# Two weight sums of a fast matrix product move from VectorE into accumulating transfers

## The chip, the cores and the metric

The kernel runs on one core of one Trainium2 chip. A core has TensorE (PE, matrix products into PSUM), VectorE (DVE), ScalarE (ACT), GpSimd (POOL) and SyncE (SP); SP issues most transfers, POOL the accumulating ones, and 16 DMA engines carry them all. The metric is the device time of one execution in microseconds. Before the change the median of three runs is 2101.67 us (2101.33 to 2106.94).

## The reference

One encoder layer on 512 tokens of width 2048, all in float32:

```
xn   = rms_norm(x)
proj = xn @ w_in                               # 2048 x 5120: conv value, gate, q, k, v
y_c  = silu(layer_norm(dwconv31(val * sigmoid(gate))))
y_n  = neighbourhood attention(q, k, v)        # 8 x 64 grid, window 8 x 16, 16 heads
x    = x + concat(rms_norm(y_c), rms_norm(y_n)) @ w_out
xn   = rms_norm(x)
up   = dwconv3(xn @ w_up)                      # 2048 x 11264
gate, val = split(up)
x    = x + (silu(gate) * val) @ w_down         # 5632 x 2048
out  = rms_norm(x)
```

The change touches only how `xn @ w_up` gets its weights.

## The kernel before, in words

**Layout.** Activations stand transposed: 16 tiles of 128 channels by 512 tokens. Every weight comes in units of 128 partitions x 1024 columns (512 KB), which are eight 128x128 blocks. For float32 accuracy, `parts` (L106) cuts each raw unit in two: ACT rounds it into `whi` (L109), VectorE forms the remainder `wlo` (L110). `mm3` (L117) then does three matmuls per block: high by high (L120), high by low (L121), low by high (L122). A unit is thus 24 matmuls.

**Stages.** The input projection (tiles `pj`) runs with convolution and attention beside it, then the output projection (`po`), then the gated MLP, then the last down products with the final norm. In the MLP the up projection is `up(f)` (L581), for 44 columns f in 11 chunks of four. For each f it forms 128 gate channels and 128 value channels for all 512 tokens at once. This is a 2x2 block product by seven multiplications instead of eight (Strassen-Winograd): the inner dimension is cut in halves, the 512 tokens in halves of 256, and the weights of f in four quarters, A11, A21, A22, A12, each one unit of 512 KB in HBM. The activation's combinations (`comb`, L485 to L516) are made once. The weights' combinations are made for each f by `factors` (L528): product 0 uses A22, product 1 uses A21 + A22, product 2 uses A21 + A11, product 3 uses A11, product 4 uses s = A21 + A22 + A11, product 5 uses A12, and product 6 uses s + A12 (signs are in the activations and in the negated value path `fwn`). So there are four additions of quarters per f, all on VectorE: L539, L541, L546, L550, each over 128x1024 numbers. `up` adds the seven products (PSUM tiles `pu`) with ACT (L602, L606) and VectorE (L605 to L611); `hidden` multiplies by the norm's factor (L627, L628), does the width-3 convolution `conv3` (L619 to L621), silu (L630) and the gate product (L631).

**Down products.** While chunk c runs up, the down projection of chunk c-1 runs between its products: `down` (L640) takes a unit of `w_down` for two output tiles; ACT copies each PSUM tile `pd` to `pdc` (L649), and POOL adds it to the residual in HBM by an accumulating transfer (`x2d`, L650). `down_units` (L559) says after which product: in the chunks 1 to 9 one unit after product 3 and one after product 6, so that a column is nine units; in chunk 0 there are none, and in the last chunk none in its first column.

**Order and buffers.** `plan` is the list of all weight units in the order of use, each a function that makes its parts; `weights()` (L141) hands out the next one and makes units three ahead (`AHEAD`). Raw units and sums share one pool of seven tiles (tag `raw`, `NR`), the parts have four tiles each (`NW`). Products 0 to 5 share three PSUM tiles (`psm`), product 6 has one of its own. The instructions of each engine are put in order by a planner from the program's order and estimated durations; on the chip each engine runs its own list in order and waits on semaphores, and a transfer's issue stands in its queue's order (SP's or POOL's) until its buffer is free.

Of the kernel before, what the change touches and what calls it, by code (L numbers as in the profile page):

```python
# [13 lines left out]
ALU = mybir.AluOpType  # L14
AX = mybir.AxisListType

P = 128
# [17 lines left out]
U = 8  # L35
# [8 lines left out]
NT = 79  # L44
NR = 7
AHEAD = 3
NW = 4
NEG = -1.0e30

# [15 lines left out]
def layer(ctx: ExitStack, tc: tile.TileContext, xT, w_in, w_out, w_up, w_down, par, tab, out):  # L65
    nc = tc.nc
# [19 lines left out]
    def t4(shape, name):  # L86

        return wpool.tile(shape, F32, tag="raw", name=name, bufs=NR)
# [13 lines left out]
    def raw_unit(src, n):  # L102
        raw = t4([P, U * P], "raw")
        return raw, nc.sync.dma_start(raw[:, :n], src)

    def parts(raw, n):  # L106
        hi = wpool.tile([P, U * P], F32R, tag="whi", name="whi", bufs=NW)
        lo = wpool.tile([P, U * P], F32R, tag="wlo", name="wlo", bufs=NW)
        i = nc.scalar.activation(hi[:, :n], raw[:, :n], AF.Copy)  # L109
        j = nc.vector.tensor_sub(lo[:, :n], raw[:, :n], hi[:, :n].bitcast(F32))  # L110
        return hi, lo, i, j
# [27 lines left out]
    plan, made = [], []  # L139

    def weights():  # L141
        at = weights.at
        weights.at += 1
        while len(made) < min(at + 1 + AHEAD, len(plan)):
            made.append(plan[len(made)]())
        return made[at]

    weights.at = 0

# [56 lines left out]
    for k in range(KD):  # L206
# [6 lines left out]
        if k in (0, 2, 6, 15):  # L213
            raw, i = raw_unit(first[len(early)], U * P)
# [8 lines left out]
    for step in ORDER:  # L223
        i = next(a_ if step == "a" else q_)
# [18 lines left out]
    def project(n):  # L243
        ps = psm.tile([P, S], F32, tag="mm", name="pj")
        for u in range(KD // U):
            w = weights()
            for k in range(U):
                kk = u * U + k
                m = mm3(ps, w, k, xs[kk][0], xs[kk][1], kk == 0, kk == KD - 1)
            tick(m)  # L250
            while late:
                late.pop()()
        return ps
# [200 lines left out]
    def out_half(m, read):  # L454
        for d in range(KD):
            w = weights()
            ps = psm.tile([P, S], F32, tag="mm", name="po2")
            for k in range(U):
                i = mm3(ps, w, k, m[k][0], m[k][1], k == 0, k == U - 1)
            tick(i)  # L460
            read(d, ps)
# [66 lines left out]
    def factors(f):  # L528

        def load(q):  # L530
            a[q] = raw_unit(w_up[f, q], U * P)[0]
            return a[q]

        def make(c):
            if c == 0:
                return load(A22)
            if c == 1:
                a["s"] = t4([P, U * P], "ws")
                add(a["s"], load(A21), a[A22])  # L539
            elif c == 2:  # L540
                add(a[A21], a[A21], load(A11))  # L541
                return a[A21]
            elif c == 3:
                return a[A11]
            elif c == 4:
                add(a["s"], a["s"], a[A11])  # L546
            elif c == 5:
                return load(A12)
            else:
                add(a["s"], a["s"], a[A12])  # L550
            return a["s"]

        a = {}
        return [lambda c=c: parts(make(c), U * P)[:2] for c in range(7)]

    A11, A21, A22, A12 = range(4)
    add = nc.vector.tensor_add
# [13 lines left out]
    for c in range(NCH):  # L571
        for i in range(CH):
            for at, make in enumerate(factors(c * CH + i)):
                plan.append(make)
                for d0 in down_units(c, i, at):
                    plan.append(lambda c=c, d0=d0: unit(down_weights((c - 1) * CH, d0), U * P))
# [4 lines left out]
    def up(f, between):  # L581

        def product(c):
            w = weights()
            ps = (psa.tile([P, S], F32, tag="po", name="pu") if c == 6 else
                  psm.tile([P, S], F32, tag="mm", name="pu"))[:, :H]
            for k in range(U):
                m = comb[c][k]
                i = mm3(ps, w, k, m[:, :H], m[:, H:], k == 0, k == U - 1)
            tick(i)  # L590
            between(c)
            return ps
# [78 lines left out]
    ws = []  # L671
# [89 lines left out]
```

## Time and profile before

| | |
|---|---|
| runs | 2101.67 us median (2101.33 to 2106.94) |
| profiled execution | span 2106.4 us |
| TensorE | 2067.0 us busy, 98% |
| VectorE | 1575.8 us busy, 75% |
| ScalarE | 988.8 us busy, 47% |
| GpSimd | 140.1 us busy, 7% |
| chain of waits | TensorE 96%, VectorE 2%, DMA 1%, ScalarE 1% |
| transfers | 270.89 MB, mean 129 GB/s |

The profile is one execution. "Busy" of TensorE counts pipelined matmuls whose ends are modelled. A row of instruction groups gives line, engine, operation, output and inputs with their sizes, the count, the busy time, the mean ns of one, and the idle time of the engine just before, with what ended it. In the timeline, `[3.05 <-DMA raw<-in_w_up]` says that the engine stood 3.05 us before this instruction and that the named thing let it go. PEclk is the granted TensorE clock, 1.00 at full speed.

### The profile page before, as it was taken

The numbers are of one execution on the slowest core, as the hardware profiler recorded it, in microseconds if no ns is written. First come the engines' busy times: TensorE is split into PE (matmuls) and PEld (weight loads), VectorE is DVE, ScalarE is ACT, GpSimd is POOL, SyncE is SP. The second block draws the span as 40 slices with busy tenths as digits, with TensorE's granted clock in tenths as the row PEclk, the third lists the DMA queues.
The fourth block names the chain that finished last, engine by engine and source line by source line (L and its number), as shares of the span: only waits on it lengthen the run. The fifth ranks groups of instructions, "written<-read, shape, count | busy, mean of one in ns | idle before, by whom it ended". The sixth has DMA issues, their size and how long they took to land.

```text
span 2106.4 us, 32366 instructions
## 1 busy us (share of the span) xinstructions
PE 2067.0 (98%) x13024; PEld 1853.7 (88%) x13024; DVE 1575.8 (75%) x2137; ACT 988.8 (47%) x1472; POOL 140.1 (7%) x166
## 2 busy tenths in 40 slices
PE   8999999999999999999999999999999999999997
PEld 6888888877878899999999999999999999998986
DVE  7986796686568897777777777777776777768666
ACT  6144424456436554454544544454454445444442
POOL 0000000000000001110111101101001011010110
PEclk9999999999999999999999999999999999999998
DMA  6233223236224235565565555556656556553672
GB/s 226 90 121 100 92 89 105 99 108 213 97 96 135 80 121 135 127 138 141 122 142 138 135 136 141 130 131 145 138 127 141 141 131 131 140 135 99 145 203 81
DMA packets 95910, 270.89 MB, mean 129 GB/s; under 512 B 10640, under 2 KB 14736, under 8 KB 95760
## 3 DMA queue, kind: packets, MB, share of 16 engines
q1 hardware_dynamic: 72720, 226.88, 34.4%
q0 software_dynamic: 23040, 41.95, 14.4%
q8 instruction: 102, 1.67, 0.3%
q14 instruction: 48, 0.39, 0.1%
HBM read 218.46 MB, written 50.33 MB: 128 GB/s over the span
## 4 chain that ended last, share of the span: by engine, by line
PE 96%; DVE 2%; DMA 1%; ACT 1%; issue 0%; SPq 0%; DVEq 0%; ACTq 0%
PE pu L120 14%; PE pu L122 14%; PE pu L121 14%; PE pd L122 8%; PE pd L120 8%; PE pd L121 8%; PE pj L120 7%; PE pj L122 7%; PE pj L121 7%; PE po L120 3%; PE po L121 3%; PE po L122 3%; PE sc L366 1%; PE po L409 1%; PE trp L396 1%; DMA raw<-in_w_up 1%
## 5 line engine op out<-in xcount | busy, mean ns | idle before, releaser
L110 DVE TENSOR_TENSOR wlo<-raw,whi 128x1024 fp32r<-128x1024 f32 x368 | 449.3, 1222 | 361.8 <-ACT whi L109 336.6
L120 PE MATMUL pu<-xc,whi 128*128 128x256 f32 x2464 | 699.8, 284 | 8.2 <-ACT vv L602 4.7
L122 PE MATMUL pu<-xc,wlo 128*128 128x256 f32 x2464 | 699.5, 284 | 0.0
L121 PE MATMUL pu<-xc,whi 128*128 128x256 f32 x2464 | 699.5, 284 | 0.0
L109 ACT ACTIVATE whi<-raw 128x1024 fp32r<-128x1024 f32 x368 | 389.2, 1059 | 627.7 <-PE pj L121 217.1
L120 PEld LDWEIGHTS pu<-xc,whi 128*128 128x128 f32 x2464 | 474.5, 193 | 12.8 <-ACT vv L602 4.9
L121 PEld LDWEIGHTS pu<-xc,whi 128*128 128x128 f32 x2464 | 474.6, 193 | 3.5 <-issue 0.4
L122 PEld LDWEIGHTS pu<-xc,wlo 128*128 128x128 f32 x2464 | 474.5, 193 | 0.0
L650 POOL DMA_DIRECT2D x2d<-pdc x160 | 139.4, 873 | 1902.0 <-ACT pdc L649 1794.1
L120 PE MATMUL pj<-xh,whi 128*128 128x512 f32 x640 | 254.0, 398 | 7.7 <-ACT whi L109 7.7
L120 PE MATMUL pd<-hh,whi 128*128 128x512 f32 x640 | 250.3, 391 | 1.9 <-ACT pdc L649 1.9
L122 PE MATMUL pj<-xh,wlo 128*128 128x512 f32 x640 | 250.6, 392 | 0.7 <-DVE wlo L110 0.6
L121 PE MATMUL pj<-xl,whi 128*128 128x512 f32 x640 | 251.2, 393 | 0.0
L121 PE MATMUL pd<-hl,whi 128*128 128x512 f32 x640 | 250.3, 391 | 0.0
L122 PE MATMUL pd<-hh,wlo 128*128 128x512 f32 x640 | 248.9, 391 | 0.0
L109 ACT ACTIVATE whi<-ws 128x1024 fp32r<-128x1024 f32 x132 | 139.9, 1060 | 192.9 <-PE pu L121 135.1
L280 DVE SCALAR_TENSOR_TENSOR y<-ch,prm,y 128x507 f32<-128x507 f32 (+14 forms) x240 | 170.1, 741 | 3.1
L110 DVE TENSOR_TENSOR wlo<-ws,whi 128x1024 fp32r<-128x1024 f32 x132 | 161.3, 1222 | 12.4 <-ACT whi L109 11.8
L649 ACT ACTIVATE pdc<-pd 128x512 f32<-128x512 f32 x160 | 94.0, 588 | 133.4 <-PE pd L122 133.3
L120 PEld LDWEIGHTS pj<-xh,whi 128*128 128x128 f32 x640 | 120.8, 189 | 36.1 <-ACT whi L109 9.0
L122 PEld LDWEIGHTS pj<-xh,wlo 128*128 128x128 f32 x640 | 120.7, 189 | 27.7 <-DVE wlo L110 2.1
L122 PEld LDWEIGHTS pd<-hh,wlo 128*128 128x128 f32 x640 | 120.3, 188 | 28.1 <-DVE wlo L110 3.4
(141 smaller groups left out, 2452.7 us busy)
## 6 DMA issues: line engine op xcount, KB each, us to landing
raw<-in_w_up SPq DMA_DIRECT2D x176, 512.0 KB, 3.5
raw<-in_w_down SPq DMA_DIRECT2D x88, 512.0 KB, 4.0
raw<-in_w_in SPq DMA_DIRECT2D x80, 512.0 KB, 3.7
x2d<-pdc POOLq DMA_DIRECT2D x160, 256.0 KB, 4.7
raw<-in_w_out SPq DMA_DIRECT2D x32, 512.0 KB, 3.4
x<-in_xT SPq DMA_DIRECT2D x32, 256.0 KB, 6.0
tab<-in_tab SPq DMA_DIRECT2D x32, 256.0 KB, 4.0
x2d<-x SPq DMA_DIRECT2D x16, 256.0 KB, 2.0
```

The lines of the kernel that those rows point to most:

```text
L109: i = nc.scalar.activation(hi[:, :n], raw[:, :n], AF.Copy)
L110: j = nc.vector.tensor_sub(lo[:, :n], raw[:, :n], hi[:, :n].bitcast(F32))
L120: nc.tensor.matmul(ps, hi[:, a], mh, start=start, stop=False)
L121: nc.tensor.matmul(ps, hi[:, a], ml, start=False, stop=False)
L122: return nc.tensor.matmul(ps, lo[:, a], mh, start=False, stop=stop)
L280: nc.vector.scalar_tensor_tensor(y[:, a:b], h[:, a + j - PAD:b + j - PAD], prm[:, o + j:o + j + 1], y[:, a:b], op0=ALU.mult, op1=ALU.add)
L366: m = nc.tensor.matmul(both[:, j, i, :], q[hp, b * P:(b + 1) * P], grid(k, KC0[b], KW)[hp], start=True, stop=True)
L396: m = nc.tensor.transpose(ps[:, 2 * i + ch, :], s[:, i, ch * P:(ch + 1) * P], ident)
L409: m = nc.tensor.matmul(grid(po, b * BLK, BLK)[hp], vt[b // 2][:, 2 * (b % 2) + ch, hp], pts[j][:, 2 * i + ch, :], start=(ch == 0), stop=(c ...
L649: nc.scalar.activation(t, ps, AF.Copy)
L650: nc.gpsimd.dma_start(xd[d], t, accum_op=ALU.add)
```

## The change

Two of the four additions are no longer done on VectorE: A21 + A22 (L539, for product 1) and A21 + A11 (L541, for product 2). In their place one quarter is loaded into a raw tile by SP, and POOL issues a second transfer from HBM that adds the other quarter to the tile in SBUF. Both are begun eight units ahead of the product that uses them (`FAR`), by a table `sums` that `weights()` looks up. Product 1 splits the summed tile directly, and the additions for product 4 (L546, now L556) and product 6 (L550, now L560) go on in the same tile on VectorE. Since the tiles of A22 and A11 are no longer shared with the additions, A22 and A11 are loaded a second time as plain operands. So a column loads five quarters plainly, where it loaded four, and adds two by accumulating transfers. Seven raw tiles are allocated per column with down units, as before (there, one of them for `ws`).

```
+FAR = 8
     def weights():
         at = weights.at
         weights.at += 1
+        for i in range(at, min(at + 1 + FAR, len(plan))):
+            sum_ = sums.pop(i, None)
+            if sum_ is not None:
+                sum_()
         while len(made) < min(at + 1 + AHEAD, len(plan)):
             made.append(plan[len(made)]())
         return made[at]
+
+    sums = {}
...
+        def summed(q1, q2):
+            t = load(q1)
+            nc.gpsimd.dma_start(t, w_up[f, q2], accum_op=ALU.add)
+            return t
+
         def make(c):
             if c == 0:
                 return load(A22)
             if c == 1:
-                a["s"] = t4([P, U * P], "ws")
-                add(a["s"], load(A21), a[A22])
+                return a["s"]
             elif c == 2:
-                add(a[A21], a[A21], load(A11))
                 return a[A21]
             elif c == 3:
-                return a[A11]
+                return load(A11)
             elif c == 4:
                 add(a["s"], a["s"], a[A11])
             elif c == 5:
...
         a = {}
+
+        def ahead(c):
+            a["s" if c == 1 else A21] = summed(*((A22, A21) if c == 1 else (A21, A11)))
+
+        for c in (1, 2):
+            sums[len(plan) + c] = lambda c=c: ahead(c)
         return [lambda c=c: parts(make(c), U * P)[:2] for c in range(7)]
```

## The prediction

> **What bounds the kernel now.** I read the page first, then stretches of the span, then the few places where TensorE stood. The page gives the engine times, the DMA queues and the issues:
>
> ```profile
> span 2106.4 us, 32366 instructions
> PE 2067.0 (98%) x13024; PEld 1853.7 (88%) x13024; DVE 1575.8 (75%) x2137; ACT 988.8 (47%) x1472; POOL 140.1 (7%) x166
> q1 hardware_dynamic: 72720, 226.88, 34.4%
> q0 software_dynamic: 23040, 41.95, 14.4%
> x2d<-pdc POOLq DMA_DIRECT2D x160, 256.0 KB, 4.7
> raw<-in_w_up SPq DMA_DIRECT2D x176, 512.0 KB, 3.5
> ```
>
> TensorE is busy 98% of the span and VectorE 75%. The stretches tell more (columns: us; busy time of PE, PEld, DVE, ACT, POOL; granted TensorE clock; DMA share; GB/s):
>
> ```profile
> 708.00:712.00 4.00, 0.54 (x4) 0.23 (x2) 3.90 (x13) 1.41 (x3) 0.00 (x0) 1.00 0.09 14
> 712.83:716.24 3.41, 3.41 (x16) 3.15 (x15) 0.79 (x2) 0.60 (x1) 0.00 (x0) 0.50 0.60 210
> 1916.00:1921.00 5.00, 0.40 (x4) 0.19 (x2) 5.00 (x8) 3.36 (x7) 0.00 (x0) 1.00 0.37 105
> 1921.15:1924.56 3.41, 3.41 (x16) 3.41 (x17) 3.41 (x5) 0.16 (x1) 0.00 (x0) 0.50 0.00 0
> 2021.00:2025.00 4.00, 2.09 (x10) 1.40 (x9) 3.68 (x7) 3.27 (x6) 0.57 (x1) 1.00 0.99 354
> 1200.00:1400.00 200.00, 200.00 (x1387) 187.21 (x1387) 145.48 (x171) 94.86 (x125) 22.63 (x26) 1.00 0.59 136
> ```
>
> ```profile
> 700.00:2000.00 1300.00, 1291.76 (x9076) 1214.77 (x9075) 979.40 (x1167) 628.16 (x839) 132.37 (x152) 1.00 0.56 132
> ```
>
> In the steady part (1200 to 1400) TensorE is busy all 200 us at the full clock. VectorE does 145 us of work beside it, so nothing that VectorE is spared there can come off the time. In all of 700 to 2000, the up projection's stage, TensorE is idle for 1300 - 1291.76 = 8.24 us. Two stops make up nearly all of it:
>
> ```profile
> 707.97 0.28 PE L122 MATMUL pu<-xc,wlo 128*128 128x256 f32 x1
> 711.71 0.39 PE L120 MATMUL pu<-xc,whi 128*128 128x256 f32 x1 [3.46 <-ACT whi L109]
> ```
>
> ```profile
> 1916.12 0.28 PE L122 MATMUL pu<-xc,wlo 128*128 128x256 f32 x1
> 1921.09 0.56 PE L120 MATMUL pu<-xc,whi 128*128 128x256 f32 x1 [4.70 <-ACT vv L602]
> ```
>
> After each stop the clock stands at 0.50 for 3.41 us (the rows 712.83 and 1921.15 above), which loses half of that, 1.71 us. The most the stage can give back is therefore 8.24 + 2 x 1.71 = 11.7 us.
>
> **What is removed: 88 of the 176 additions on VectorE.** These are the two groups below (columns: count, busy us, mean ns, idle before). Their sum is 107.3 us of VectorE time:
>
> ```profile
> L541 DVE TENSOR_TENSOR raw<-raw 128x1024 f32<-128x1024 f32 x44 | 53.7, 1221 | 4.7 <-DMA raw<-in_w_up 4.7
> L539 DVE TENSOR_TENSOR ws<-raw 128x1024 f32<-128x1024 f32 x44 | 53.6, 1219 | 3.1 <-DMA raw<-in_w_up 3.1
> ```
>
> In the steady part this is worth nothing: TensorE covers it, with 54.5 us of idle VectorE in 200. It is worth something at the two stops.
>
> *The stop at 1916.* Here a column (one turn f of the up projection) without down units begins, and the loads come late. From the timeline of SP, VectorE and ACT:
>
> ```profile
> 1883.14 25.43 SPq L104 DMA_DIRECT2D raw<-in_w_up  x5
> ```
>
> ```profile
> 1903.25 1.23 DVE L539 TENSOR_TENSOR ws<-raw 128x1024 f32<-128x1024 f32 x1 [3.05 <-DMA raw<-in_w_up]
> 1913.20 1.22 DVE L541 TENSOR_TENSOR raw<-raw 128x1024 f32<-128x1024 f32 x1 [4.38 <-DMA raw<-in_w_up]
> 1917.46 0.74 DVE L621 SCALAR_TENSOR_TENSOR uy<-vl,fwn,uy 128x511 f32<-128x511 f32 x1
> ```
>
> ```profile
> 1917.64 0.63 ACT L630 ACTIVATE uy<-uy 128x512 f32<-128x512 f32 x1 [5.64 <-DVE uy L621]
> 1920.68 0.63 ACT L602 ACTIVATE vv<-pu 128x256 f32<-128x256 f32 x2
> ```
>
> VectorE stood 3.05 us before L539 and 4.38 us before L541, each time for a load of one operand. ACT runs in order: its L630 waited 5.64 us for VectorE, and the evacuation L602 queued behind it, for which TensorE stopped. Both waits belong to the removed additions. The start-to-start gap is 1921.09 - 1916.12 = 4.97 us, less 0.12 us for one matmul: 4.85 us lost, and 1.71 us at half clock after it. Without the additions nothing on VectorE waits for those operands, and the two engines have 7.4 us more in hand than the stop was long. I count the whole: **-6.56 us**. What could be late next is a split (L109, L110) whose tile has not landed. By the instruction order of the two programs, 129 of the 264 loads of the stage go out one to three weight units before VectorE needs them; in the changed program nearly all plain loads go out five to seven units ahead and the summed tiles about twelve. A unit of 24 matmuls at 0.12 us is 2.88 us, so five units are 14 us against the 3.5 us of the page's median landing. So I take no new stop.
>
> *The stop at 708.* It ends when ACT's split (L109) of the first column's last sum is done, behind VectorE's queue. One L541 of the next column lies in that queue:
>
> ```profile
> 702.04 1.22 DVE L541 TENSOR_TENSOR raw<-raw 128x1024 f32<-128x1024 f32 x1
> 703.17 0.42 DVE L514 SCALAR_TENSOR_TENSOR t<-t,b 128x256 f32<-128x256 f32 x1
> 709.28 1.22 DVE L550 TENSOR_TENSOR ws<-ws,raw 128x1024 f32<-128x1024 f32 x1
> ```
>
> L514 moves up by 703.17 - 702.04 = 1.13 us, and with it the combinations of x that everything after waits for: **-1.13 us**. The rest of the stop, 3.46 - 1.13 = 2.3 us, stays, and I leave its half-clock stretch in place.
>
> The Trainium skill, "TensorE: Matmul & The Clock Gate", section "What's actually happening", says that the clock halves after an idle window of about 3.4 us and returns after a busy one. The 3.41 us stretches at 0.50 agree with the window, and the stop near 2022 (4.00 - 2.09 = 1.91 us idle) kept clock 1.00. By that rule a stop of 2.3 us would not close the gate, and the sum would be 1.7 us lower.
>
> **What is added.** Each column reloads one quarter plainly (44 loads of 512 KB on SP) and adds two quarters by transfers from POOL's queue (88 of 512 KB). ACT's work is unchanged, and VectorE reads the same tiles.
>
> *Queues.* SP spends 0.33 us on an issue:
>
> ```profile
> 1205.48 0.33 SPq L104 DMA_DIRECT2D raw<-in_w_up  x1
> ```
>
> 44 x 0.33 = 15 us over 1300 us, in time when SP waits for buffers anyway (waits of the DMA queue: us in total, times, longest):
>
> ```profile
> SPq L104 <- DVE wlo L110: 1638.3, 338, 19.5
> ```
>
> POOL takes 0.873 us for one accumulating issue, and it idles most of the span:
>
> ```profile
> L650 POOL DMA_DIRECT2D x2d<-pdc x160 | 139.4, 873 | 1902.0 <-ACT pdc L649 1794.1 <-ACT uu L606 95.2 <-DMA raw<-in_w_down 12.7
> ```
>
> 88 x 0.873 = 77 us go into 1902 us of idle. The new wait is POOL's: a sum waits there for its plain load. Queued behind it are the x2d transfers of the down projection, whose results are wanted only after the last column. The reverse also holds, so a sum waits for the pdc evacuation ahead of it. In the order, the pair of sums of a column stands at the first and second x2d transfer of one down unit, and the ACT splits that read them come after those of the same down unit one column later. A column lasts 31.08 us:
>
> ```profile
> 1199.62 0.69 DVE L631 TENSOR_TENSOR uy<-uy 128x512 f32<-128x512 f32 x1
> 1230.70 0.68 DVE L631 TENSOR_TENSOR uy<-uy 128x512 f32<-128x512 f32 x1
> ```
>
> So a sum has over 31 us to land, where the 256 KB accumulations land in 4.7 us (page). Cost: nothing. If that cover went, each late sum would stop TensorE by its lateness, up to 88 times.
>
> *DMA engines.* No sum into SBUF is in the trace, so I bound it. q1: 34.4% of 2106.4 us for 226.88 MB is 1.67 us for a 512 KB load. q0: 14.4% of 2106.4 us over 160 transfers is 1.90 us for 256 KB accumulated in HBM. A 512 KB sum costs the engines between 1.90 us (the price goes by rows, 128 in both) and 9.4 us (they are held for the whole landing, 2 x 4.7). I take 3.79 us, by bytes, since an accumulation of the same kind is the nearest row. Per column now: 6 loads and 4 accumulations, 10.0 + 7.6 = 17.6 us of 31.08, 57% (the stretch shows 0.59). After: 7 x 1.67 + 7.6 + 2 x 3.79 = 26.9 us, 86%. Columns without down units last 7 x 2.88 = 20.2 us and need 5 x 1.67 + 7.6 = 15.9 us, 79%. The engines keep up: cost nothing, with longer landings that the five-unit lead covers.
>
> *Buffers.* Seven raw tiles serve seven allocations a column, as before, but two are held for more than a column. The leads counted above already contain this.
>
> **Sum.** -6.56 - 1.13 = -7.7 us: the profiled execution would go from a span of 2106.4 to 2098.7 us. That execution is 4.7 us above the median of the runs, 2101.67 us (2101.33 to 2106.94), and I take the same difference off the median: **2094.0 us**, 0.37% faster. About 0.3%, 6.3 us, is what a measurement of this kernel can tell from no change.
>
> **Rivals.**
>
> *The stops give back less (no change).* The profiled execution is like the longest run, and the two shorter ones lie 5.3 us below it. They may lack some of the half-clock stretches, which are 1.71 us each. Then the gain is 6.0 us (2095.7). Or SP's late loads at 1883 to 1908 stay late, and the split takes over the wait of the addition: of the 4.85 us only part is saved, 2097 to 2101.7 us. For it: those loads wait for buffers, and the buffers are as many as before. Against: the leads in the order.
>
> *The DMA engines become the bound (slower).* Per column they have 31.08 - 11.7 - 7.6 = 11.8 us for two sums, so this decides from 5.9 us a sum on. At 7.6 us, twice my price, a column takes 34.5 us, 3.4 us more in each of 36 columns with down units: +122 us, about 2224 us. At the upper bound of 9.4 us it is +250 us. For it: the share goes from 0.59 to 0.86 already by my price. Against: the same kind of addition costs only 1.13 times a load of twice its size, and a stretch of 0.99 share moved 354 GB/s (2021 to 2025).
>
> The Trainium skill, "DMA: Bandwidth & Descriptors", section "Issuing engines are not separate DMA queues", says that transfers of all issuing engines run on the same 16 engines and interleave. It speaks for this rival, since POOL's queue then brings no bandwidth of its own; no run here shows where the engines saturate.
>
> *Single late sums (slower).* If sums land in time on average but some do not, for instance where the first columns' sums share seven tiles with the last w_out units (600 to 700 us), TensorE stops there: four stops of 4 us with their half-clock stretches, less the gain, give +15 us, 2117 us.
>
> *The clock gate stays open after 708* (the rule above): 9.4 us less, 2092.3 us.
>
> **How the numbers follow.** The forecast, with the gate variant: 0.56. Less is given back: 0.31, of which nearly all lies within 0.3%. The DMA engines bind: 0.08. Single late sums: 0.05. Faster by over 0.3% is then 0.56, within 0.31, slower 0.13. Low end: the gate variant less the 1.9 us stop at 2022, 2090.4, and a little for the spread of runs: 2089. High end: no gain, 2101.7, and half of the 5 us by which runs differ: 2104. The slower cases, 0.13, are left out.
>
> **What would show it.** Right: no stop of TensorE near 1916 and no half clock there; the stop at 708 about 1.1 us shorter; VectorE busy about 107 us less; POOL's issues 248; a DMA share of 0.8 to 0.9 in the steady part with TensorE still at 200 of 200 us. Wrong: splits (L109 there) that wait for accumulating transfers, a column longer than 31.08 us, accumulated 512 KB that cost over 5.9 us of the engines, or a new stop between 600 and 720 us.

## The result, and the profile after

The changed kernel takes 2097.82 us, median of 12 runs (2095.68 to 2099.91). In the same comparison the kernel before takes 2102.14 us (2100.98 to 2108.62, 12 runs). The ratio is 0.9976, 95% interval 0.9968 to 0.9983: 0.24% faster, about 4.3 us. The forecast was 2094.0 us with a range of 2089 to 2104.

The page of the kernel after, the lines that answer to those of before:

```profile
span 2098.1 us, 32752 instructions
PE 2064.4 (98%) x13024; PEld 1851.4 (88%) x13024; DVE 1485.3 (71%) x2049; ACT 990.9 (47%) x1472; POOL 217.8 (10%) x254
q1 hardware_dynamic: 79056, 249.95, 35.7%
q0 software_dynamic: 35712, 88.10, 24.9%
raw<-in_w_up SPq DMA_DIRECT2D x220, 512.0 KB, 4.0
raw<-in_w_up POOLq DMA_DIRECT2D x88, 512.0 KB, 5.5
x2d<-pdc POOLq DMA_DIRECT2D x160, 256.0 KB, 5.5
```

Stretches of the kernel after (us; busy time of PE, PEld, DVE, ACT, POOL; granted clock; DMA share; GB/s):

```profile
700.00:2000.00 1300.00, 1297.58 (x9146) 1220.94 (x9146) 900.43 (x1091) 634.55 (x846) 206.52 (x236) 1.00 0.75 184
1200.00:1400.00 200.00, 200.00 (x1388) 187.26 (x1387) 131.77 (x157) 94.48 (x125) 34.12 (x39) 1.00 0.76 183
1916.00:1921.00 5.00, 5.00 (x44) 5.00 (x44) 4.41 (x6) 2.28 (x3) 0.00 (x0) 1.00 0.30 105
```

VectorE does 90.5 us less. The two removed groups held 107.3 us, but a group's duration counts the overlap of neighbouring instructions twice. The 88 sums land in 5.5 us (median), and POOL issues 88 + 160 = 248 transfers. In the steady part TensorE is busy 200 of 200 us as before, and the DMA share is 0.76. At 1916 TensorE does not stop. It idles 2.42 us in all of 700 to 2000, against 8.24 us in the profiled execution before, and nearly all of the 2.42 us is the stop that was at 708. TensorE's matmuls around it, in the kernel after:

```profile
709.12 0.28 PE L123 MATMUL pu<-xc,wlo 128*128 128x256 f32 x1
711.80 0.58 PE L121 MATMUL pu<-xc,whi 128*128 128x256 f32 x1 [2.40 <-ACT whi L110]
```

From start to start that is 2.68 us, where it was 3.74 us (707.97 to 711.71): 1.06 us less.

Read alone, the two profiles say that the span went from 2106.4 to 2098.1 us, -8.3 us, close to the -7.7 us of the prediction's sum. The medians say -4.3 us. The experiments begin with this difference.

### The profile page after: what moved, and what is told of

Its sections match the earlier page's. It is cut to its first block, busy times and chain, and to the rows that moved or that the text cites. A ratio compares the mean times of both kernels' runs of the same rounds, so it can differ in the third digit from the quotient of the medians.

```text
span 2098.1 us, 32752 instructions
## 1 busy us (share of the span) xinstructions
PE 2064.4 (98%) x13024; PEld 1851.4 (88%) x13024; DVE 1485.3 (71%) x2049; ACT 990.9 (47%) x1472; POOL 217.8 (10%) x254
## 3 DMA queue, kind: packets, MB, share of 16 engines
q1 hardware_dynamic: 79056, 249.95, 35.7%
q0 software_dynamic: 35712, 88.10, 24.9%
## 4 chain that ended last, share of the span: by engine, by line
PE 96%; DVE 2%; ACT 1%; DMA 1%; issue 0%; SPq 0%; DVEq 0%; ACTq 0%
PE pu L121 14%; PE pu L123 14%; PE pu L122 14%; PE pd L121 8%; PE pd L122 8%; PE pd L123 8%; PE pj L121 7%; PE pj L123 7%; PE pj L122 7%; PE po L121 3%; PE po L122 3%; PE po L123 3%; PE sc L373 1%; PE po L416 1%; PE trp L403 1%; DMA raw<-in_w_in 1%
## 5 line engine op out<-in xcount | busy, mean ns | idle before, releaser
L111 DVE TENSOR_TENSOR wlo<-raw,whi 128x1024 fp32r<-128x1024 f32 x500 | 610.2, 1221 | 455.8 <-ACT whi L110 429.6
L110 ACT ACTIVATE whi<-raw 128x1024 fp32r<-128x1024 f32 x500 | 529.3, 1060 | 835.5 <-PE pu L122 302.0
L543 POOL DMA_DIRECT2D raw<-in_w_up x88 | 77.7, 883 | 1040.4 <-DVE xc L498 637.9
L121 PEld LDWEIGHTS pd<-hh,whi 128*128 128x128 f32 x640 | 120.5, 188 | 24.9 <-ACT pdc L665 2.3
```

The lines of the kernel that those rows point to most:

```text
L121: nc.tensor.matmul(ps, hi[:, a], mh, start=start, stop=False)
L543: nc.gpsimd.dma_start(t, w_up[f, q2], accum_op=ALU.add)
```

## The experiments

Times are medians. The first four kernels ran together, beside a kernel before of 2103.45 us; the next four beside 2101.78 us; the last four beside 2102.84 us. "Drift" below means this: matmul by matmul, by their number in the program, how much one kernel's starts gain on those of the kernel before (its second profile) between 716 and 1800 us.

### 1. The kernel before, once more

No edit.

> The kernel before, unchanged, once more, for a second profiled execution. The profiled execution of before (span 2106.4 us) belongs to its long executions, so what is asked is whether the stop at 1916 stands in an ordinary one too. Theory (the stop is there in every execution, since late loads make it, and only the half-clock stretches of 1.71 us each come and go): ratio 1.000, the profile has TensorE idle for 4 to 5 us near 1916 after L602, and executions differ by 1.7 to 3.4 us with the granted clock. Rival (the stop comes and goes with the execution): a profile with a shorter span, near 2100 us, has no stop near 1916, and then the gain of the change in ordinary executions must come from somewhere else.

Measured: 2101.7 us (2101.21 to 2104.74, 11 runs), ratio 0.9993 (0.9985 to 1.0002). The span of its profile is 2099.8 us, 6.6 us below the first profile of the same program, and the stop at 1916 is not there. A stretch of this second execution:

```profile
700.00:2000.00 1300.00, 1296.45 (x9128) 1218.84 (x9127) 985.34 (x1175) 631.59 (x844) 132.39 (x152) 1.00 0.53 133
```

3.55 us of idle TensorE are left, the stop near 708. The same two additions and the same two ACT instructions, in this execution:

```profile
1899.92 1.22 DVE L539 TENSOR_TENSOR ws<-raw 128x1024 f32<-128x1024 f32 x1
1908.23 1.23 DVE L541 TENSOR_TENSOR raw<-raw 128x1024 f32<-128x1024 f32 x1 [2.75 <-DMA raw<-in_w_up]
1912.68 0.63 ACT L630 ACTIVATE uy<-uy 128x512 f32<-128x512 f32 x1 [0.88 <-DVE uy L621]
1915.73 0.63 ACT L602 ACTIVATE vv<-pu 128x256 f32<-128x256 f32 x2
```

L539 does not wait (3.05 us before), L541 waits 2.75 us (4.38 us), ACT's L630 0.88 us (5.64 us). The two executions part in the transfers issued between 1893 and 1916, first in the first profile, then in the second (KB each, median us from issue to landing):

```profile
raw<-in_w_up SPq DMA_DIRECT2D x2, 512.0 KB, 6.1
```

```profile
raw<-in_w_up SPq DMA_DIRECT2D x2, 512.0 KB, 3.6
```

In the first profile the load issued at 1895.87 landed after 7.3 us, in the second its counterpart after 3.8 us. L539 waited for it, the splits queued behind L539 gave their buffer back late, and the next load went out at 1908.24, 3.3 us later than in the second execution. An accumulating transfer to HBM was issued 0.4 us before this load in both executions; it landed after 7.8 us in the first and after 5.5 us in the second. So it is not what the two differ in, and why both transfers were late in the first is not shown.

What follows: the stop is real, the waits were read rightly, but an ordinary execution doesn't have it. It is no part of the median.

### 2. Transfer-made sums in two columns only

```
+FEW = (1, 41)
...
             if c == 1:
+                if f not in FEW:
+                    a["s"] = t4([P, U * P], "ws")
+                    add(a["s"], load(A21), a[A22])
                 return a["s"]
             elif c == 2:
+                if f not in FEW:
+                    add(a[A21], a[A21], load(A11))
                 return a[A21]
             elif c == 3:
-                return load(A11)
+                return load(A11) if f in FEW else a[A11]
...
-        for c in (1, 2):
+        for c in (1, 2) if f in FEW else ():
```

> Only columns 1 and 41 have their two sums made by accumulating transfers (4 transfers in place of 88); the other 42 columns add on VectorE as before. Column 1 has the L541 at 702.0 us, column 41 the L539 and L541 at 1903 and 1913 us, for which VectorE stood. Theory (the gain is the two stops and nothing else): the whole gain stays, ratio 0.996 to 0.998, no stop near 1916, the one at 708 about 1.1 us shorter, with VectorE busy only about 5 us less than before. Rival (the gain is spread over the columns, because VectorE has 107 us less to do): 4 of 88 transfers give 4 of 88 parts, ratio 0.9995 to 1.000.

Measured: 2100.03 us (2098.51 to 2103.68), ratio 0.9987 (0.9978 to 0.9996). The stop at 708 is 2.68 us long, as in the full change; nothing near 1916. Between these places TensorE's starts keep the distance of the kernel before: no drift.

What follows: taking the additions of column 1 off VectorE is enough to shorten the stop at 708. What is missing to the full change lies in the other columns and in the clock (below).

### 3. The kernel before with eight raw tiles

```
-NT = 79
-NR = 7
+NT = 77
+NR = 8
```

> The kernel before with eight raw tiles in place of seven (and 77 of the small tiles in place of 79); all sums stay on VectorE. Theory (the stop at 1916 is late loads, and they are late because the tiles are taken): the loads go out earlier, no stop near 1916, 4 to 6 us less, ratio 0.997 to 0.998, without any accumulating transfer. Rival (it is VectorE's load that makes the stop, the additions themselves being too many where no down unit spaces them): the stop stays, ratio 0.9995 to 1.000.

Measured: 2098.62 us (2095.95 to 2102.6), ratio 0.9980 (0.9971 to 0.9989). All four sums stay on VectorE. Its stretch 700 to 2000:

```profile
700.00:2000.00 1300.00, 1297.57 (x9147) 1220.85 (x9146) 993.52 (x1174) 633.55 (x846) 132.40 (x152) 1.00 0.53 133
```

VectorE works 993.5 us there, 93 us more than in the changed kernel, and TensorE is as busy as there (1297.57 against 1297.58 us). The stop at 708 is 2.68 us, and the drift is 0.76 us. VectorE's order at that stop is another one than before:

```profile
702.50 0.42 DVE L510 SCALAR_TENSOR_TENSOR t<-b,t 128x256 f32<-128x256 f32 x1
702.96 0.43 DVE L514 SCALAR_TENSOR_TENSOR t<-t,b 128x256 f32<-128x256 f32 x1
```

No L541 stands between the two, as it did in the kernel before, and none up to L550.

What follows: one more raw tile, and the order that the planner makes with it, give nearly the whole gain without a single transfer-made sum.

### 4. The sums eight units ahead, but on VectorE

```
         def summed(q1, q2):
             t = load(q1)
-            nc.gpsimd.dma_start(t, w_up[f, q2], accum_op=ALU.add)
+            add(t, t, raw_unit(w_up[f, q2], U * P)[0])
             return t
```

> The changed kernel with the two sums begun eight units ahead as there, but made on VectorE from two plain loads in place of one load and one accumulating transfer. It separates the early start from the move off VectorE. Theory: the early start alone removes the stop near 1916 (no operand is late), so 4 to 6 us less; VectorE keeps its 176 additions, so the stop at 708 stays as long as before (3.5 us), and the columns without down units (720 to 790 us), where VectorE is nearly always busy, may show small stops of under 2 us: ratio 0.9975 to 0.9995. Rival (the engine is what matters): the stop near 1916 stays, ratio 1.000 or above.

Measured: 2101.22 us (2098.83 to 2103.61), ratio 0.9991 (0.9982 to 0.9999). No stop near 1916. The stop at 708 is 3.52 us, followed by two half-clock windows; near 797 the starts lose 0.45 us on the kernel before, and from 801 to 1800 they gain 0.9 us.

What follows: the drift comes without the transfers, here too. The stop at 708 stays long where an addition stands in VectorE's queue ahead of the last splits (one, at 706.70, does here); experiment 3 shows that it also goes where the additions stay on VectorE, but elsewhere in its order.

### 5. The changed kernel once more

No edit.

> The changed kernel once more, beside the runs below. Lead theory (the gain comes from loads that go out earlier; what VectorE is spared is worth nothing by itself, except at the stop near 709): 2097 to 2099 us, TensorE's starts 0.8 to 1.0 us ahead of the unchanged kernel's by 1668 us, a stop of 2.68 us near 709, none near 1910. Rival (the difference between the two kernels is that of the batches): 2100 to 2102 us.

Measured: 2097.84 us (2096.8 to 2099.95, 8 runs), ratio 0.9976 (0.9966 to 0.9986), as before. The stop near 709 is 2.68 us again, but no half-clock stretch follows it. What the drift is shows in TensorE's waits, first of the kernel before (second profile), then of the one after (us in total, times, longest):

```profile
PEld pd L122 <- DVE wlo L110: 3.5, 8, 0.4
```

```profile
PEld pu L121 <- ACT vv L618: 2.7, 8, 0.3
```

Before, eight weight loads of the down products wait 0.4 us each for a split. After, eight others wait 0.3 us each. The drift is 0.84 us in the first profile of the changed kernel and 0.80 us in this one, in eight steps of about 0.1 us, one in each chunk. Another 0.2 us are gained near 1916.

### 6. VectorE gets its work back, on the summed tiles

```
             if c == 1:
+                nc.vector.tensor_tensor(a["s"], a["s"], a["s"], op=ALU.max)
                 return a["s"]
             elif c == 2:
+                nc.vector.tensor_tensor(a[A21], a[A21], a[A21], op=ALU.max)
```

> The changed kernel, but VectorE gets its work back: at the two places where the additions stood, it takes the maximum of the summed tile with itself (88 instructions of 128x1024, about 1.22 us each, 107 us), which changes no value. Their operands have been under way for eight units. Lead theory: the time stays within 1.5 us of the changed kernel's (2097 to 2099.5 us); only the stop near 709 goes back to about 3.5 to 3.74 us, because one such instruction again stands ahead of L514; no stop near 1910; the gain of 0.8 to 1.0 us over 716 to 1668 stays. Rival (VectorE's spared 107 us are the gain): the time goes back to the unchanged kernel's, 2101 to 2104 us, and the gain over 716 to 1668 is gone.

Measured: 2135.04 us (2129.9 to 2138.85), ratio 1.0148 (1.0129 to 1.0167). Neither theory gave that. The wait is new and it is VectorE's, for the sums (us in total, times, longest; then one of them, with the wait before it):

```profile
DVE raw L550 <- DMA raw<-in_w_up: 169.9, 41, 7.3
```

```profile
922.56 1.23 DVE L550 TENSOR_TENSOR raw<-raw 128x1024 f32<-128x1024 f32 x1 [6.27 <-DMA raw<-in_w_up]
```

The planner put each maximum directly behind its sum in VectorE's order, not three units before the use. VectorE reaches L550 3.1 us (median) after POOL issued the sum, which lands after 6.6 us, and stands there, with everything else queued behind it; TensorE then stops at some ten places, by 1 to 5 us.

What follows: the run doesn't separate VectorE's time from the lead, as it brought a wait of its own. It prices that wait at 37 us: in the changed kernel the sums cost nothing because their first reader comes late.

### 7. The sums three units ahead

```
-FAR = 8
+FAR = 3
```

> The changed kernel with the sums begun three units ahead in place of eight. Lead theory: a plain load lands in 4.0 us, the sum behind it in 5.5 us more, POOL's issue is 0.88 us: 10.4 us, and the two splits come after; three units of 24 matmuls are 8.6 us. Each sum then is some 2 to 4 us late, at least once a column: 44 x 2 to 4 us, 2185 to 2275 us, with splits (L110) that wait for accumulating transfers. Rival (SP and POOL run ahead as far as buffers allow, so the written lead counts for little): 2098 to 2102 us.

Measured: 2097.77 us (2095.78 to 2100.29), ratio 0.9975 (0.9965 to 0.9986). The rival was right. From POOL's issue of a sum to the start of the first split that reads it there are 15.2 to 35.3 us (median 19.2 us, 88 sums); with eight units they are 23.8 to 59.1 us (median 32.5). The sums land in 6.1 us there and in 5.5 us with eight units (medians), so both are enough. The written distance is only the least: the planner and the free buffers put the issues further ahead.

What follows: "begun eight units ahead" earns nothing over three.

### 8. All four sums by transfers

```
             elif c == 4:
-                add(a["s"], a["s"], a[A11])
+                nc.gpsimd.dma_start(a["s"], w_up[f, A11], accum_op=ALU.add)
...
             else:
-                add(a["s"], a["s"], a[A12])
+                nc.gpsimd.dma_start(a["s"], w_up[f, A12], accum_op=ALU.add)
```

> The changed kernel with the third and fourth sum of a column made by accumulating transfers as well (88 more issues on POOL; these two are begun three units ahead, onto a tile whose splits have to be done first). By the price that the changed kernel's page gives, 2.49 us of the engines for one sum, a column takes 7 x 1.57 + 4 x 1.90 + 4 x 2.49 = 28.6 us of 31.08: the engines keep up at a share near 0.92, and what is lost is only the wait of a sum in its chain (issue 0.88 us and landing 5.5 us against 8.6 us of lead less the two splits): 2098 to 2130 us. By the price of the prediction, 3.79 us, a column takes 33.8 us: 2.7 us more in each of 36 columns, 2190 us or more, with the DMA share at 1.0 in the steady part.

Measured: 2134.29 us (2129.34 to 2134.98), ratio 1.0141 (1.0125 to 1.0157). Its queue row, steady stretch and wait:

```profile
q0 software_dynamic: 48384, 134.24, 34.9%
1200.00:1400.00 200.00, 200.00 (x1388) 187.26 (x1387) 118.86 (x147) 93.00 (x125) 45.70 (x52) 1.00 0.89 218
ACT whi L110 <- DMA raw<-in_w_up: 313.4, 70, 8.8
```

Between this kernel and the changed one, q0 grows from 24.9% of 2098.1 to 34.9% of 2133.2 us, by 222 us for 88 more sums: 2.52 us of the engines for a sum (experiment 12 gives 2.96 us). At a share of 0.89 TensorE still runs 200 of 200 us in the steady part, so the engines keep up. The loss is in the chain: ACT stands 313 us for sums that could begin only after the splits of the tile they add to, and TensorE stops at some ten places, by 1 to 6 us each, six of them with half clock behind. The time lies just above the 2130 us of the theory's range, and far under the 2190 us of the rival.

What follows: two sums of a column have a lead, the other two have none. The change takes the right two.

### 9. VectorE gets its work back, on a scratch tile

```
-NT = 79
+NT = 77
...
+    prev_hi = [None]
+    idle = consts.tile([P, U * P], F32, name="idle")
...
+        prev_hi[0] = hi
         return hi, lo, i, j
...
             if c == 1:
+                add(idle, idle, prev_hi[0].bitcast(F32))
                 return a["s"]
             elif c == 2:
+                add(idle, idle, prev_hi[0].bitcast(F32))
                 return a[A21]
```

> The changed kernel, but VectorE gets 88 additions of 128x1024 on a scratch tile (about 1.22 us each, 107 us), one behind the split of the unit before each transfer-made sum; they wait for no transfer and nothing waits for them (two tiles of the t pool make room). Buffer theory (the gain comes from raw tiles that are filled earlier, VectorE's time is worth nothing): 2097 to 2099 us, TensorE's starts still 0.8 to 1.0 us ahead of the unchanged kernel's by 1668 us, VectorE near 1592 us, no stop near 1910. Rival (the spared VectorE time is the gain): 2100.5 to 2103 us, and the short waits of TensorE's weight loads for wlo (3.5 us in 8 in the unchanged kernel) come back.

Measured: 2101.62 us (2099.04 to 2104.07), ratio 0.9992 (0.9983 to 1.0001). The gain is gone, as the rival's time has it, but not in the way of the rival: the eight waits for `wlo` don't come back, and between 801 and 1800 the starts gain on the kernel before as the changed kernel's do (from 2.4 to 1.5 us behind it). The loss has one place, TensorE's stop near 796:

```profile
797.94 0.50 PE L128 MATMUL pd<-hh,wlo 128*128 128x512 f32 x1 [1.59 <-DVE wlo L115]
```

This is the end of the four columns without down units. VectorE's load there, in the kernel before (second profile) and after:

```profile
717.00:797.00 80.00, 80.00 (x663) 79.67 (x662) 77.03 (x96) 43.94 (x57) 0.00 (x0) 1.00 0.29 99
```

```profile
717.00:797.00 80.00, 80.00 (x663) 79.67 (x662) 70.33 (x90) 44.60 (x57) 5.22 (x6) 1.00 0.64 171
```

77.03 of 80 us before and 70.33 after. With the scratch additions TensorE's starts fall back there by 1.9 us.

What follows: VectorE's spared time is worth nothing where down units stand between the products. In the columns without them the scratch additions cost 1.9 us in this order. How busy VectorE is doesn't decide it: the kernel before has no stop there with 77.03 us, the one with eight tiles none with 76.15 us and all additions, and this kernel stops with 73.83 us. What its place in the order does was not separated further. The rest of the distance to the changed kernel is half-clock time.

### 10. The changed kernel with eight raw tiles

```
-NT = 79
-NR = 7
+NT = 77
+NR = 8
```

> The changed kernel with eight raw tiles in place of seven (and two tiles fewer in the t pool). If both the transfers and the eighth tile only take the same late loads out of the way, nothing is left for the second of them: 2097 to 2098.5 us, the same stops near 590, 709 and 2014. Rival (the two gains are of different places and add up): 2094 to 2096 us.

Measured: 2097.89 us (2096.98 to 2100.73), ratio 0.9976 (0.9966 to 0.9986), with the stops near 590, 708 (2.68 us) and 2012. The transfers and the eighth tile take away the same losses; together they give no more than the change alone. No kernel of this study beats the changed one by more than the spread.

### 11. The kernel before with six raw tiles

```
-NR = 7
+NR = 6
```

> The unchanged kernel with six raw tiles in place of seven. Buffer theory (the lead of the loads is set by the number of raw tiles, and the stop near 1916 is a load too late by chance at a place with no lead): with a tile fewer the stop near 1905 to 1925 is there in the profile, at 5 us or more with a half-clock stretch, and the waits of VectorE for loads of w_up grow over the unchanged kernel's 2.8 to 7.8 us: 2106 us or more. Rival (the lead does not depend on the tiles): 2101 to 2104 us, and no such stop.

Measured: 2103.11 us (2099.35 to 2106.73), ratio 0.9997 (0.9988 to 1.0006), and no stop near 1916. The waits for loads did grow, and other waits went:

```profile
DVE raw L541 <- DMA raw<-in_w_up: 45.4, 38, 1.8
PEld pu L120 <- ACT vv L602: 3.0, 9, 0.3
```

38 waits of about 1.2 us, and the time stays. The stop at 708 is 3.87 us long. The eight waits for `wlo` of experiment 5 are gone, nine for L602 stand in their place, and the drift is 0.82 us: as large as in the changed kernel, with later loads and every addition on VectorE.

What follows: fewer tiles make the loads later everywhere, and the work beside hides it. So the number of tiles is not what made the stop at 1916; the buffer theory, in the simple form that I tested, falls. The drift needs neither the transfers nor earlier loads: it comes with six, with seven and with eight tiles wherever the planner made a new order for the whole stage, and stays away in experiment 2, where 42 columns keep their additions. That the order is its cause is the nearest reading; no run changes the order alone.

### 12. The transfers left out

```
             t = load(q1)
-            nc.gpsimd.dma_start(t, w_up[f, q2], accum_op=ALU.add)
+            pass
             return t
```

> The changed kernel with the 88 accumulating transfers left out: the two tiles of a column hold a plain quarter each, so the up projection is computed with wrong weights. If the transfers cost nothing on the path, as the prediction has it: 2096.5 to 2098.5 us, the same stops, a DMA share near 0.60 in the steady part in place of 0.76. Rival (their traffic or POOL's queue holds something up, such as the loads of the last columns): 1 us or more below the changed kernel, with the stop near 2014 shorter than 2.3 us.

This kernel leaves the two sums out and multiplies with plain quarters, so it computes other values. Measured: 2098.15 us (2095.26 to 2100.65), ratio 0.9975 (0.9966 to 0.9984). Steady stretch and queue row:

```profile
1200.00:1400.00 200.00, 200.00 (x1388) 187.26 (x1387) 131.79 (x157) 94.84 (x125) 22.62 (x26) 1.00 0.58 152
q0 software_dynamic: 23040, 41.95, 12.5%
```

The DMA share falls from 0.76 to 0.58 and the time doesn't move: the 88 sums and their POOL issues cost nothing on the path, as predicted. From this kernel to the changed one q0 grows from 262 to 522 us, 2.96 us for a sum; with experiment 8 the price is 2.5 to 3.0 us.

### Half-clock time

Each execution comes with its span and its mean granted clock (three decimals, so 1 us at this span). Span times clock is called the full-clock part here; the rest is half of the time at half clock. In the 14 profiles 5.2 to 7.3 us of this rest belong to the end of the kernel, where TensorE has little left to do. In the mean over 81 executions of the kernel before the parts are 2090.7 and 10.8 us; over 20 of the kernel after they are 2088.8 and 7.4 us. So in the mean the change takes 5.2 us: about 1.9 us of stops and waits and about 3.3 us of half-clock time. The first agrees with 1.06 us at the stop near 708, 0.8 us of drift and 0.2 us near 1916. The second is about two stretches of 1.71 us less in each execution. The split is rough, by about 1 us: the kernel of experiment 2 has no drift, and its full-clock part comes out at 2088.3 us, below that of the full change.

In the 14 profiles the stop near 708 to 709 was followed by half clock in all four where it is 3.5 to 3.9 us long, and in five of eight where it is 2.68 us. The same stop, in the profile after and in the changed kernel's second one (stretches of 3.41 us):

```profile
708.19:711.60 3.41, 1.21 (x11) 1.01 (x9) 3.31 (x11) 0.91 (x1) 0.00 (x0) 1.00 0.01 2
711.60:715.02 3.42, 3.22 (x9) 2.19 (x10) 2.11 (x4) 1.29 (x4) 0.00 (x0) 0.50 0.74 253
```

```profile
707.01:710.42 3.41, 1.83 (x16) 1.63 (x14) 3.34 (x8) 0.70 (x2) 0.00 (x0) 1.00 0.00 0
710.42:713.83 3.41, 2.59 (x16) 2.11 (x17) 2.70 (x7) 1.91 (x4) 0.00 (x0) 1.00 0.54 178
713.83:717.24 3.41, 3.41 (x31) 3.41 (x30) 0.69 (x1) 1.33 (x2) 0.86 (x1) 1.00 0.57 157
```

Half clock begins and ends on a grid of 3.413 us that each execution has at another offset (after: 711.60 - 592.14 = 119.46 = 35 x 3.413). In the first profile the stop lies in one window, which is busy for 1.21 us only, and the next window is at 0.50. In the second the grid cuts the same stop in two; the windows are busy 1.83 and 2.59 us, and the clock stays. By the idle time of such rows (3.41 us less TensorE's busy time) the border lies at about 1.9 us in one window: of the windows with a single stop, all with 1.90 us or more were followed by half clock, none with 1.84 us or less, and of two with 1.88 us one was. At the very end of the kernel, where products of one column stand in the window, 1.5 to 1.7 us were enough.

A stop can also cost a second window. The stop near 590 of the kernel after:

```profile
588.73:592.14 3.41, 0.88 (x4) 0.38 (x2) 3.41 (x5) 1.67 (x2) 0.00 (x0) 1.00 0.47 156
592.14:595.55 3.41, 2.41 (x6) 1.95 (x7) 3.38 (x7) 0.00 (x0) 0.00 (x0) 0.50 0.48 154
595.55:598.97 3.42, 3.42 (x10) 2.65 (x9) 0.57 (x1) 0.00 (x0) 0.00 (x0) 0.50 0.00 0
```

TensorE idles 1.0 us in the first window at half clock, and the next one is at 0.50 too. Over the 14 profiles half clock went on where such a window had 0.85 us or more of idle, and ended where it had 0.60 us or less. So a shorter stop gains twice, by its length and by the half-clock windows that it causes. With these two borders, and every offset of the grid as likely as another, a stop of 3.46 us (the wait before) is followed by 1.16 half-clock windows in the mean and one of 2.40 us (the wait after) by 0.60. The difference, 0.56 x 1.71 us, is about 1.0 us of the 3.3 us, an estimate. The rest, some 2 us, is not traced and stays open.

## Why the prediction was right or wrong

**The sign, and the range: right.** The time fell, inside the range; the fall of 0.24% is under the 0.3% of the likeliest case. That the forecast came as near as 3.8 us is in part luck, as the next points show.

**The stop at 1916, -6.56 us: the failed step.** The waits and their chain were read rightly, and no profile of the changed kernel has the stop. But the kernel before doesn't have it in every execution. The step that failed is the assumption "I take the same difference off the median". The first profile was of one of the longest executions: a span of 2106.4 us against 2099.8 us in the second, and among the 81 executions only three have a full-clock part of at least 2093.8 us, which is what that profile comes to. The prediction had written down the sign of it, that two of three runs lay 5.3 us below the longest, and used it for half-clock stretches alone. It also compared a span with run times: here a run's time is 1.8 us above its span (2099.91 against 2098.1 us), so the profiled execution lay 6.5 us above the median, not 4.7. In an ordinary execution this term is about zero.

**The stop at 708, -1.13 us: right**, -1.06 us measured, and experiment 2 shows that taking the sums of column 1 off VectorE is enough for it. Experiment 3 shows that it isn't the only way: VectorE's order does it too.

**The gate after 708: partly.** The sum left the half-clock stretch in place; of the stops of 2.68 us three in eight had none behind them. The rival with the open gate was the right mechanism with the wrong certainty. The Trainium skill, "TensorE: Matmul & The Clock Gate", section "What's actually happening", says that the window runs freely, independent of the kernel's start. The grid above agrees. Its idle window of about 3.4 us as the condition doesn't agree: 1.9 us of idle inside one window were enough here.

**What the sum left out:** 0.8 us of drift, 0.2 us near 1916 and about 3.3 us of half-clock time. These and the 1.06 us are the gain of the means, 5.2 us (4.3 us between the medians); in the sum the term at 1916 stood in their place, and so -7.7 us came out with the right sign, at 1.8 times the fall of the median, for a wrong reason. About 2 us of the half-clock time have no traced cause.

**VectorE's time, "worth nothing" in the steady part: right there**, by the drift of experiment 9 and by experiment 3. The columns without down units have no part in the sum; the scratch additions of experiment 9 cost 1.9 us there.

**The leads: right in the order, not in the cause.** Sums were to have over 31 us; they have 23.8 to 59.1 us, median 32.5. But 15.2 to 35.3 us do as well (experiment 7), and in experiment 11 late loads cost nothing. So earlier loads are not what the gain needs: the drift came with later ones too.

**The price of a sum: mis-sized, without effect.** Taken at 3.79 us, measured 2.5 to 3.0 us (experiments 8 and 12), so the DMA share is 0.76 and not 0.86. The border of 5.9 us was far, and experiment 12 shows that the sums cost nothing. The rivals of binding DMA engines and of late sums didn't come about; experiments 6 and 8 show what sums cost whose reader stands close: 36 to 37 us.

**The rival "the stops give back less"** began rightly, with 2095.7 us: the profiled execution is like the longest run, the ordinary ones have less to give back. What they lack is not only a half-clock stretch, as it said, but the stop at 1916 itself.

## What to carry to other kernels

Before a stop in one profile is counted, ask whether the ordinary execution has it: if the profiled execution is some us longer than the median, the stop may be the reason, and a second profile of the same program is the cheapest experiment there is. A change that also moves the order of the instructions needs a kernel beside it that moves the order alone: here one raw tile more gave nearly the same gain. Work moved to accumulating transfers is free as long as its first reader stands far enough behind in its engine's order; with a reader close behind them such transfers cost 36 to 37 us here. At 98% TensorE what is left are stops of 1 to 4 us, and each is worth its length plus up to 1.71 us for every half-clock window it causes.

## What was not expected of the hardware

- An accumulating transfer into SBUF costs the DMA engines less by bytes than one into HBM: 2.5 to 3.0 us for 512 KB (experiments 8 and 12), against 1.90 us for 256 KB (the rows of before; 1.64 us in the kernel without the sums, 12.5% of 2098.7 us for 160) and 1.57 us for a plain load of 512 KB (q1 of the page after, 35.7% of 2098.1 us for 249.95 MB).
- A single load of 512 KB that lands in 3.5 to 4 us as a rule took 7.3 us once, and at a place without reserve that made a stop of 4.85 us and a half-clock stretch. The cause of the late landing is not shown.
- The clock halves by windows of 3.413 us that run freely, from about 1.9 us of idle in one window on: a stop of 3.92 us near 590 was followed by half clock in 12 of 14 profiles (in four of them for two windows), one of 2.68 us in five of eight, one of 2.3 us near the end in two of thirteen.
